# Attention in pairs of query blocks and gate products over the whole array in a hybrid decoder step

## The chip, the cores and the metric

The kernel runs on one core of one Trainium2 chip. The metric is the device time of one execution in microseconds (us). Three runs of the kernel before gave 1314.17, 1315.66 and 1316.99 us (median 1315.66 us).

## What is computed

One step of a hybrid decoder layer, for a prompt of 1024 tokens and eight single new tokens, all in float32. The input is normalised and multiplied with a wide weight `w_in`, and the columns of the product are split up:

```
xn = rms_norm(x, norm_pre)
u, z_rnn, q, k, v, z_attn, g_rnn, g_attn = split(xn @ w_in)
uc = causal_conv(u)                                   # four taps
r, i = sigmoid(uc @ w_a + b_a), sigmoid(uc @ w_x + b_x)   # 16 diagonal blocks of 64 channels
h = linear scan over time of (a(r), b(r, i, uc))
y_rnn = (h * silu(z_rnn)) @ w_rnn_out
for g, (window, dilation) in enumerate(((128, 1), (512, 4), (2048, 16))):
    o[g], lse[g] = dilated causal attention with linear biases, query blocks of 128
y_attn = (merge of o by lse * silu(z_attn)) @ w_attn_out
out = x + rms_norm((sigmoid(g_rnn) * y_rnn + sigmoid(g_attn) * y_attn) @ w_out, norm_post)
```

The eight new tokens go the same way, with caches of keys and values. There are 3 attention groups, 8 heads of 64 channels in each, and 1024 recurrent channels.

## The kernel before, in words

**Projections.** `w_in` is taken in pieces of 128 columns. A projection (`project`, L409) computes one piece for all 1032 tokens in three chunks of 256, 384 and 392 columns (`CHUNKS`). To keep float32 accuracy with the faster fp32r matmul, weights and inputs are split into a high and a low part, and each chunk is 8 x 3 matmuls (`mm3`, L389: high by high, high by low, low by high) into one PSUM tile of the tag `pj`. ScalarE or VectorE reads the chunk out of PSUM (the `evac` functions) and so frees the tile. The weights of the next pieces are loaded by DMAs of 512 KB, issued from SyncE, and split by ScalarE (L225) and VectorE (L226).

**Lanes.** TensorE works through the projections in a fixed order, and other work is slipped in between. That other work is written as Python generators in lanes: the recurrence (`chain`, L601), the attention (L778), its merge, the new tokens (`sample`). The emitting program keeps a clock, `clk`, that adds up what it thinks each matmul costs. After each half of a chunk `tick` (L109) lets every lane whose due time has come emit one step. A step ends with `yield N`, and its lane is due again N ns later. So the order on every engine is set when the program is written out, and each half chunk of 12 matmuls is followed by a visit of some lanes, or of none.

**Slots.** Most SBUF tiles come from an arena of `NSLOT` slots of equal size. Weights are loaded ahead only as far as slots are free. Where a needed slot isn't free, `Arena.get` (L53) forces the lanes on (`force`, L117), due or not, until one is.

**PSUM.** `ps_tile` (L81) gives 8 banks of 512 columns: 3 to `pj`, 3 to `s`, 1 to `pt`, 1 to `o`.

**The gate products** (`chain_front`, L553). For each block of 128 channels and each half `s` of it, the tile `xs[s]` holds 64 channels' high parts on 64 partitions and their low parts on the other 64. The product with the high weights `lh` runs over all 128 partitions; the one with the low weights `ll` uses only the 64 partitions of the high parts. Both add into one `s` tile, and ScalarE takes two sigmoids from it (L591). A step emits all three chunks of one half, six matmuls: 16 such steps in all, four for each of the four chains.

**Attention** (L778). One pass for each group and pair of heads, 12 in all, each over 8 query blocks. `scores` multiplies the queries of a block with one or two key blocks for both heads, each head over its 64 partitions, into two `s` tiles; VectorE adds the bias and takes the minimum (L802), ScalarE the exponential (L806). `turn` transposes the result into a `pt` tile, which is copied out by VectorE or ScalarE (L820, L822). `values` multiplies with the values, each head into 64 output partitions (128 by 64 in the rows). One step does one block: `scores` of block b, `turn` of block b-2, `values` of block b-4, with the first two and two later steps also turning rows of v and k. Steps are 1700 ns of `clk` apart:

```
for b in range(8 + 2 * LAG):
    if LAG <= b < 8 + LAG:
        turn(b - LAG)
    if b < 8:
        scores(b)
    if b >= 2 * LAG:
        values(b - 2 * LAG)
```

Of the kernel before, what the change touches and what calls it, by code (L numbers as in the profile page):

```python
# [22 lines left out]
DIL = (1, 4, 16)  # L23
# [6 lines left out]
NSLOT = 43  # L30
# [3 lines left out]
LAG, STEP = 2, 1700  # L34
# [5 lines left out]
def f32(ap):  # L40
    return ap.bitcast(F32)
# [28 lines left out]
def hybrid_step(ctx: ExitStack, tc: tile.TileContext, I, O):  # L70
# [10 lines left out]
    def ps_tile(tag):  # L81
        bufs = {"pj": 3, "s": 3, "pt": 1, "o": 1}[tag]
        return psum.tile([128, 512], F32, tag=tag, bufs=bufs, name="ps_" + tag)
# [64 lines left out]
    def tr(out, in_, idn):  # L148
        clk[0] += 109
        nc.tensor.transpose(out, in_, idn)  # L150
# [401 lines left out]

    def chain_front(b, X, R, T):  # L553
# [3 lines left out]
        ll = small.tile([128, 256], F32R, tag="t2", name="ll")  # L557
        nc.scalar.activation(lh, lw, AF.Copy)
        nc.vector.tensor_tensor(ll, lw, f32(lh), op=OP.subtract)
# [21 lines left out]
        for s in range(2):  # L581
            rows = slice(64 * s, 64 * s + 64)
            ws = slice(128 * s, 128 * s + 128)
            for c0, n in CHUNKS:
                p = ps_tile("s")
                cs = slice(c0, c0 + n)
                mm(p[:, :n], lh[:, ws], xs[s][:, cs], start=True, stop=False)
                mm(p[:, :n], ll[rows, ws], xs[s][rows, cs], start=False, stop=True)
                for gate in range(2):
                    at = 64 * (gate ^ s)  # L590
                    nc.scalar.activation(G[gate][rows, cs], p[at:at + 64, :n], AF.Sigmoid,  # L591
                                         bias=par[rows, b, 5 + gate:6 + gate])
            yield 1500
# [184 lines left out]
    def attention(g, hp):  # L778
# [14 lines left out]
        def scores(b):  # L793
            k0, n = keys(b)
            pt = P[b] = small.tile([128, 2, 256], F32, tag="P", name="P", bufs=LAG + 1)
            base = C["base2"] if g == 2 else C["base0"][:, 256 - 128 * n:256]
            for h in range(2):
                p = ps_tile("s")
                hs = slice(64 * h, 64 * h + 64)
                mm(p[:, :128 * n], qt[hs, 128 * b:128 * b + 128], kt[hs, 128 * k0:128 * (k0 + n)],  # L800
                                 start=True, stop=True)
                nc.vector.tensor_tensor_reduce(out=pt[:, h, :128 * n], in0=p[:, :128 * n], in1=base,  # L802
                                               scale=-SLOPES[g][2 * hp + h] * DIL[g], scalar=3e38,
                                               op0=OP.add, op1=OP.min, accum_out=st[:, g, 0, h, b:b + 1])
            for h in range(2):
                nc.scalar.activation(pt[:, h, :128 * n], pt[:, h, :128 * n], AF.Exp, scale=-1.0,  # L806
                                     bias=st[:, g, 0, h, b:b + 1], accum_out=st[:, g, 1, h, b:b + 1])

        def turn(b):
            k0, n = keys(b)  # L810
            pt = P.pop(b)
            p = ps_tile("pt")
            for h in range(2):
                for kb in range(n):
                    tr(p[:, (h * n + kb) * 128:(h * n + kb) * 128 + 128],
                                        pt[:, h, 128 * kb:128 * kb + 128], ident)
            t = PT[b] = small.tile([128, 2 * n, 128], F32, tag="PT", name="PT", bufs=LAG + 1)
            src = p[:, :256 * n].rearrange("p (b c) -> p b c", c=128)
            if b % 2:
                nc.vector.tensor_copy(t, src)  # L820
            else:
                nc.scalar.activation(t, src, AF.Copy)  # L822

        def values(b):
            k0, n = keys(b)
            vn = vns[g, hp]
            t = PT.pop(b)
            if b % 4 == 0:
                PO[0] = ps_tile("o")
            o = PO[0]  # L830
            off = 128 * (b % 4)
            for kb in range(n):
                for h in range(2):
                    mm(o[64 * h:64 * h + 64, off:off + 128], vn[:, k0 + kb, 64 * h:64 * h + 64],
                                     t[:, h * n + kb], start=kb == 0, stop=kb == n - 1)
            if b % 4 == 3:
                f = b // 4
# [10 lines left out]
        for b in range(8 + 2 * LAG):  # L848
            if LAG <= b < 8 + LAG:
                turn(b - LAG)  # L850
            if b < 8:
                scores(b)
            if b >= 2 * LAG:
                values(b - 2 * LAG)
            if b < 2:
                v_rows(g, hp, b)
            elif 6 <= b < 8:
                k_rows(g, hp, b - 6)
            if b == 7:
                ar.free(kts.pop((g, hp)), qts.pop((g, hp)))  # L860
            if b == 7 + 2 * LAG:
                ar.free(vns.pop((g, hp)))
                if g == 2:
                    spawn("merge", merge(hp), 1000)
            yield STEP
# [300 lines left out]
    for e in started:  # L1166
        advance(e)
    C = late_consts()
# [219 lines left out]
```

## Time and profile before

| what | value |
|---|---|
| median of the three runs | 1315.66 us |
| the profiled execution's own time | 1316.49 us |
| its span in the profile | 1314.1 us |
| TensorE matmuls (PE) busy | 1294.3 us, 98% |
| TensorE weight loads (PEld) busy | 1203.1 us, 92% |
| VectorE (DVE) busy | 604.8 us, 46% |
| ScalarE (ACT) busy | 550.0 us, 42% |
| GpSimd (POOL) busy | 219.8 us, 17% |
| mean granted TensorE clock | 0.996 |

Matmuls are pipelined, so a row's duration is longer than what it costs: the cost of one in a sequence is the distance between its start and the start of the next. An fp32 product of the attention shows as two rows (two passes), an fp32r product or a transpose as one. What a timeline row merges (x4) is the stretch from its start to the next row's start.

### The profile page before, as it was taken

What the parts mean: (1) busy time and instruction counts of PE and PEld (TensorE: products, weight loads), DVE (VectorE), ACT (ScalarE), POOL (GpSimd) and SP (SyncE); (2) the same over time, 40 slices, a digit from 0 to 9 for tenths busy, and PEclk for the clock granted to TensorE, in tenths of its full rate; (3) what the DMA queues carried; (4) which work ended last, traced back from release to release, by engine and by line L of the source; (5) the groups of instructions that cost most, each with busy time, mean ns of one, the idle gap of its engine ahead of it and who ended that gap; (6) DMA issues with size and microseconds to landing.
All of it is one profiled execution on the core that took longest, in us unless ns stands there. A gap on an engine that the chain in (4) does not pass through costs nothing.

```text
span 1314.1 us, 21425 instructions
## 1 busy us (share of the span) xinstructions
PE 1294.3 (98%) x8726; PEld 1203.1 (92%) x8726; DVE 604.8 (46%) x1300; ACT 550.0 (42%) x1223; POOL 219.8 (17%) x228
## 2 busy tenths in 40 slices
PE   8999999999999999999999999999999999999996
PEld 8998999989998898888988988888989999999996
DVE  6552744827436324533345325544244245555225
ACT  6548357384574343334334333333563222122222
POOL 4001402314022002240016002140026000001001
PEclk9999999999999999999999999999999999999998
DMA  7201300423302017312354115421285356313033
GB/s 237 69 23 33 98 16 17 145 81 131 95 17 89 25 41 206 87 51 65 89 137 102 41 41 169 109 66 45 50 228 158 120 184 211 105 65 98 32 113 146
DMA packets 149303, 125.96 MB, mean 96 GB/s; under 512 B 8857, under 2 KB 135289, under 8 KB 149198
## 3 DMA queue, kind: packets, MB, share of 16 engines
q1 hardware_dynamic: 149206, 124.61, 31.6%
q8 instruction: 68, 1.11, 0.4%
q14 instruction: 29, 0.24, 0.1%
HBM read 98.44 MB, written 26.21 MB: 95 GB/s over the span
## 4 chain that ended last, share of the span: by engine, by line
PE 94%; DVE 2%; ACT 1%; issue 1%; DMA 0%; POOLq 0%; POOL 0%; SPq 0%; ACTq 0%; DVEq 0%
PE ps_pj L146 79%; PE ps_s L146 7%; PE ps_o L146 3%; PE ps_s L150 3%; PE ps_pt L150 2%; DVE ck L1036 1%; ACT P L806 0%; DMA wraw<-in_w_in 0%; DVE wlo L226 0%; DVE tanh L631 0%; ACT whi L225 0%; DVE PT L820 0%; DVE P L802 0%; POOLq L1384 0%; ACT whi L243 0%
## 5 line engine op out<-in xcount | busy, mean ns | idle before, releaser
L146 PE MATMUL ps_pj<-xh,whi 128*128 128x256 f32 (+3 forms) x1760 | 579.1, 329 | 0.0
L146 PE MATMUL ps_pj<-xh,wlo 128*128 128x256 f32 (+3 forms) x1760 | 558.1, 317 | 0.3 <-DVE wlo L239 0.3
L146 PE MATMUL ps_pj<-xl,whi 128*128 128x256 f32 (+3 forms) x1760 | 558.0, 317 | 0.0
L146 PEld LDWEIGHTS ps_pj<-xh,whi 128*128 128x128 f32 x1760 | 331.6, 188 | 22.8 <-issue 20.9
L146 PEld LDWEIGHTS ps_pj<-xl,whi 128*128 128x128 f32 x1760 | 331.8, 189 | 0.2
L146 PEld LDWEIGHTS ps_pj<-xh,wlo 128*128 128x128 f32 x1760 | 331.4, 188 | 0.5 <-DVE wlo L239 0.5
L226 DVE TENSOR_TENSOR wlo<-wraw,whi 128x512 fp32r<-128x512 f32 x176 | 152.5, 867 | 296.3 <-ACT whi L225 285.9
L806 ACT ACTIVATE P<-P,stat 128x128 f32<-128x128 f32 (+1 forms) x192 | 85.0, 443 | 123.9 <-DVE stat L802 123.8
L225 ACT ACTIVATE whi<-wraw 128x512 fp32r<-128x512 f32 x176 | 109.4, 623 | 7.6 <-DVE tanh L632 3.0
L146 PE MATMUL ps_pj<-wlo,mh 128*128 128x256 f32 (+1 forms) x288 | 79.1, 281 | 0.0
L146 PE MATMUL ps_pj<-whi,ml 128*128 128x256 f32 x256 | 72.0, 281 | 0.0
L146 PE MATMUL ps_pj<-whi,mh 128*128 128x256 f32 x256 | 72.0, 281 | 0.0
L802 DVE CUSTOM_DVE_ANT_0 P<-ps_s,base 128x128 f32<-128x128 f32 (+1 forms) x192 | 59.7, 347 | 21.6 <-PE ps_s L146 18.2
L820 DVE COPY PT<-ps_pt 128x512 f32<-128x512 f32 (+1 forms) x48 | 28.8, 600 | 87.8 <-PE ps_pt L150 49.9
L706 ACT ACTIVATE qt<-ps_pj,qsc 128x384 f32<-128x384 f32 (+1 forms) x36 | 27.4, 762 | 94.8 <-PE ps_pj L146 94.8
L146 PE MATMUL ps_s<-kt,qt 64*128 64x128 f32 (+1 forms) x384 | 59.0, 372 | 3.2 <-DVE stat L802 3.2
L146 PE MATMUL ps_pj<-hzl,whi 128*128 128x256 f32 (+2 forms) x192 | 61.5, 320 | 0.0
L146 PE MATMUL ps_pj<-hzh,wlo 128*128 128x256 f32 (+2 forms) x192 | 61.5, 320 | 0.0
L146 PE MATMUL ps_pj<-hzh,whi 128*128 128x256 f32 (+2 forms) x192 | 61.4, 320 | 0.0
L1088 ACT ACTIVATE sg<-ps_pj 128x256 f32<-128x256 f32 (+2 forms) x48 | 21.9, 457 | 92.8 <-PE ps_pj L146 90.8
L591 ACT ACTIVATE gate<-ps_s,par 64x256 f32<-64x256 f32 (+2 forms) x96 | 52.1, 542 | 13.2 <-PE ps_s L146 10.5
L146 PE MATMUL ps_o<-PT,vn 128*64 128x128 f32 x560 | 52.2, 292 | 1.3 <-ACT ot L846 1.3
(243 smaller groups left out, 1679.2 us busy)
## 6 DMA issues: line engine op xcount, KB each, us to landing
wraw<-in_w_in SPq DMA_DIRECT2D x72, 512.0 KB
ck<-in_cache_kv_w SPq DMA_DIRECT2D x24, 512.0 KB
sgd<-sg SPq DMA_DIRECT2D x16, 516.0 KB
sgl<-sgd SPq DMA_DIRECT2D x16, 516.0 KB
xin<-in_x_prompt SPq DMA_DIRECT2D x16, 512.0 KB
qb<-sd SPq DMA_DIRECT2D x12, 512.0 KB
fb<-fd SPq DMA_DIRECT2D x24, 256.0 KB
hzd<-uc SPq DMA_DIRECT2D x8, 516.0 KB
```

Of the source, the lines that this page charges most:

```text
L146: nc.tensor.matmul(out, lhsT, rhs, start=start, stop=stop)
L150: nc.tensor.transpose(out, in_, idn)
L225: nc.scalar.activation(hi[:, a:b], raw[:, a:b], AF.Copy)
L226: nc.vector.tensor_tensor(lo[:, a:b], raw[:, a:b], f32(hi[:, a:b]), op=OP.subtract)
L591: nc.scalar.activation(G[gate][rows, cs], p[at:at + 64, :n], AF.Sigmoid, bias=par[rows, b, 5 + gate:6 + gate])
L706: nc.scalar.activation(dst, src, AF.Copy, scale=C["qsc"][:, g, hp:hp + 1])
L802: nc.vector.tensor_tensor_reduce(out=pt[:, h, :128 * n], in0=p[:, :128 * n], in1=base, scale=-SLOPES[g][2 * hp + h] * DIL[g], scalar=3e38, ...
L806: nc.scalar.activation(pt[:, h, :128 * n], pt[:, h, :128 * n], AF.Exp, scale=-1.0, bias=st[:, g, 0, h, b:b + 1], accum_out=st[:, g, 1, h, ...
L820: nc.vector.tensor_copy(t, src)
L1036: nc.vector.tensor_tensor(acc, acc, t, op=OP.add)
L1088: nc.scalar.activation(z[:, c0:c0 + n], p[:, :n], AF.Sigmoid)
```

## The change

Four things change together. `scores`, `turn` and `values` take two query blocks at a time, and the loop has 6 steps instead of 12, 3400 ns apart instead of 1700; a step's `turn` handles the pair whose scores were made one step earlier (before: two steps earlier). The low gate weights lie in two standing tiles that are zero outside the two 64 by 128 quarters in use (`clear_low_w` zeroes them once), so the low product runs over all 128 partitions. The gate chunks are emitted one by one, with a `yield 1300` after each instead of a `yield 1500` after three. PSUM goes from 3 to 2 banks for `pj` and from 1 to 2 for `pt`, and the arena has 42 slots instead of 43.

```
-NSLOT = 43
+NSLOT = 42
-LAG, STEP = 2, 1700
+STEP = 3400
...
-        bufs = {"pj": 3, "s": 3, "pt": 1, "o": 1}[tag]
+        bufs = {"pj": 2, "s": 3, "pt": 2, "o": 1}[tag]
...
+    low_w = [const.tile([128, 256], F32R, name=f"low_w{i}") for i in range(2)]
...
-        ll = small.tile([128, 256], F32R, tag="t2", name="ll")
+        ll = low_w[b % 2]
         nc.scalar.activation(lh, lw, AF.Copy)
-        nc.vector.tensor_tensor(ll, lw, f32(lh), op=OP.subtract)
+        for s in range(2):
+            rows, ws = slice(64 * s, 64 * s + 64), slice(128 * s, 128 * s + 128)
+            nc.vector.tensor_tensor(ll[rows, ws], lw[rows, ws], f32(lh[rows, ws]), op=OP.subtract)
...
                 mm(p[:, :n], lh[:, ws], xs[s][:, cs], start=True, stop=False)
-                mm(p[:, :n], ll[rows, ws], xs[s][rows, cs], start=False, stop=True)
+                mm(p[:, :n], ll[:, ws], xs[s][:, cs], start=False, stop=True)
                 for gate in range(2):
                     at = 64 * (gate ^ s)
                     nc.scalar.activation(G[gate][rows, cs], p[at:at + 64, :n], AF.Sigmoid,
                                          bias=par[rows, b, 5 + gate:6 + gate])
-            yield 1500
+                yield 1300
...
+        def scores(bs):
+            ps = [ps_tile("s") for _ in range(2)]
+            for b in bs:
+                k0, n = keys(b)
+                off = 256 * (b % 2)
+                for h in range(2):
+                    hs = slice(64 * h, 64 * h + 64)
+                    mm(ps[h][:, off:off + 128 * n], qt[hs, 128 * b:128 * b + 128], kt[hs, 128 * k0:128 * (k0 + n)],
+                       start=True, stop=True)
+            for b in bs:
...
+        pairs = [(2 * i, 2 * i + 1) for i in range(4)]
+        for i in range(6):
+            if 1 <= i < 5:
+                turn(pairs[i - 1])
+            if i < 4:
+                scores(pairs[i])
+            if i >= 2:
+                values(pairs[i - 2])
+            if i < 2:
+                v_rows(g, hp, i)
+            elif i < 4:
+                k_rows(g, hp, i - 2)
...
+            yield STEP
...
+    clear_low_w()
     C = late_consts()
```

How this moves instructions shows at three places.

**TensorE, one visit of the recurrence.** `lh` and `ll` (after: `low_w`) are the high and low gate weights, `uc` the split input. Before, in the last chain:

```order
L146 MATMUL ps_pj<-xh_24_123,wlo_2710 128x256
L146 MATMUL ps_s<-uc_156_2674,lh 128x256
L146 MATMUL ps_s<-uc_156_2674,ll 128x256
L146 MATMUL ps_s<-uc_156_2674,lh 128x384
L146 MATMUL ps_s<-uc_156_2674,ll 128x384
L146 MATMUL ps_s<-uc_156_2674,lh 128x392
L146 MATMUL ps_s<-uc_156_2674,ll 128x392
L146 MATMUL ps_pj<-xh_17_116,whi_2709 128x384
```

After, an ordinary visit in the second chain:

```order
L146 MATMUL ps_pj<-xh_24_123,wlo_2125 128x256
L146 MATMUL ps_s<-uc_120_2090,lh 128x256
L146 MATMUL ps_s<-uc_120_2090,low_w_135 128x256
L146 MATMUL ps_pj<-xh_17_116,whi_2124 128x384
L146 MATMUL ps_pj<-xl_25_124,whi_2124 128x384
```

Six matmuls in one visit become two, in three visits.

**The second chain's end, where the arena has no slot left.** After the change eight pairs stand in a row here, at the end of the last `z` projection, forced by the next projection's weights. On TensorE, the first six of the eight pairs (the last two, of 392 columns, and then the next projection follow):

```order
L146 MATMUL ps_s<-uc_120_2090,lh 128x392
L146 MATMUL ps_s<-uc_120_2090,low_w_135 128x392
L146 MATMUL ps_s<-uc_125_2174,lh 128x392
L146 MATMUL ps_s<-uc_125_2174,low_w_136 128x392
L146 MATMUL ps_s<-uc_121_2091,lh 128x256
L146 MATMUL ps_s<-uc_121_2091,low_w_135 128x256
L146 MATMUL ps_s<-uc_126_2175,lh 128x256
L146 MATMUL ps_s<-uc_126_2175,low_w_136 128x256
L146 MATMUL ps_s<-uc_121_2091,lh 128x384
L146 MATMUL ps_s<-uc_121_2091,low_w_135 128x384
L146 MATMUL ps_s<-uc_126_2175,lh 128x384
L146 MATMUL ps_s<-uc_126_2175,low_w_136 128x384
```

ScalarE's part of the same place, after the change (`zs` reads a `pj` tile, each `gate` row an `s` tile):

```order
L549 ACTIVATE zs_2221<-ps_pj 128x392
L601 ACTIVATE gate_2253<-ps_s,par 64x392
L601 ACTIVATE gate_2254<-ps_s,par 64x392
L601 ACTIVATE gate_2275<-ps_s,par 64x392
L601 ACTIVATE gate_2276<-ps_s,par 64x392
L601 ACTIVATE gate_2253<-ps_s,par 64x256
L601 ACTIVATE gate_2254<-ps_s,par 64x256
L601 ACTIVATE gate_2275<-ps_s,par 64x256
L601 ACTIVATE gate_2276<-ps_s,par 64x256
```

Each `s` tile has two sigmoids to wait for, and there are three such tiles.

**TensorE, one visit of the attention** in the group with dilation 16 (one key block for each query block). Before:

```order
L146 MATMUL ps_pj<-xh_24_123,wlo_4735 128x256
L150 MATMUL ps_pt<-ident,P 128x128 x2
L146 MATMUL ps_s<-kt_4466,qt_4638 128x128 x2
L146 MATMUL ps_o<-PT,vn_4763 64x128 x2
L146 MATMUL ps_pj<-xh_17_116,whi_4734 128x384
L146 MATMUL ps_pj<-xl_25_124,whi_4734 128x384
```

After (here with a step that also turns rows of k):

```order
L146 MATMUL ps_pj<-xh_20_119,wlo_4720 128x384
L150 MATMUL ps_pt<-ident,P 128x128 x4
L146 MATMUL ps_s<-kt_4450,qt_4606 128x128 x4
L146 MATMUL ps_o<-PT,vn_4755 64x128 x4
L150 MATMUL ps_s<-ident,kt_4450 128x128 x4
L146 MATMUL ps_pj<-xh_21_120,whi_4719 128x384
```

Each visit holds twice the products, and there are half as many visits. Between two of one pass stand 24 to 36 projection matmuls after the change, 12 to 24 before.

## Rows read from the trace of the kernel before

**Rows 1.** Page, part 1: busy us (share) x instructions.
```profile
PE 1294.3 (98%) x8726; PEld 1203.1 (92%) x8726; DVE 604.8 (46%) x1300; ACT 550.0 (42%) x1223; POOL 219.8 (17%) x228
```

**Rows 2.** TensorE timeline, one gate visit: start us, us, line, out<-in, shape, xcount.
```profile
270.19 0.28 PE L146 MATMUL ps_s<-uc,lh 128*128 128x256 f32 x1
270.40 0.38 PE L146 MATMUL ps_s<-uc,ll 64*128 64x256 f32 x1
270.71 0.44 PE L146 MATMUL ps_s<-uc,lh 128*128 128x384 f32 x1
...
272.21 0.44 PE L146 MATMUL ps_pj<-xh,whi 128*128 128x384 f32 x1
272.49 0.34 PE L146 MATMUL ps_pj<-xl,whi 128*128 128x384 f32 x1
```

**Rows 3.** TensorE timeline, an attention visit with one key block.
```profile
501.62 0.34 PE L146 MATMUL ps_pj<-xh,wlo 128*128 128x392 f32 x1
501.80 0.38 PE L150 MATMUL ps_pt<-ident,P 128*128 128x128 f32 x2
502.11 0.49 PE L146 MATMUL ps_s<-kt,qt 64*128 64x128 f32 x4
502.53 0.44 PE L146 MATMUL ps_o<-PT,vn 128*64 128x128 f32 x4
502.90 0.39 PE L146 MATMUL ps_pj<-xh,whi 128*128 128x256 f32 x1
503.12 0.27 PE L146 MATMUL ps_pj<-xl,whi 128*128 128x256 f32 x1
503.23 0.28 PE L146 MATMUL ps_pj<-xh,wlo 128*128 128x256 f32 x1
```

**Rows 4.** TensorE timeline, an attention visit with two key blocks.
```profile
909.74 0.60 PE L150 MATMUL ps_pt<-ident,P 128*128 128x128 f32 x4
910.27 0.70 PE L146 MATMUL ps_s<-kt,qt 64*128 64x256 f32 x4
910.90 0.66 PE L146 MATMUL ps_o<-PT,vn 128*64 128x128 f32 x8
911.49 0.44 PE L146 MATMUL ps_pj<-xh,whi 128*128 128x384 f32 x1
911.77 0.34 PE L146 MATMUL ps_pj<-xl,whi 128*128 128x384 f32 x1
```

**Rows 5.** Timeline around 606.8 us, weight load (PEld) beside matmul.
```profile
606.77 0.19 PEld L146 LDWEIGHTS ps_pj<-xh,wlo 128*128 128x128 f32 x1
606.89 0.28 PE L146 MATMUL ps_pj<-xh,wlo 128*128 128x256 f32 x1
```

**Rows 6.** Page, part 5: busy us, mean ns of one | idle before.
```profile
L591 ACT ACTIVATE gate<-ps_s,par 64x256 f32<-64x256 f32 (+2 forms) x96 | 52.1, 542 | 13.2 <-PE ps_s L146 10.5
```

**Rows 7.** VectorE timeline, projections of `za`.
```profile
232.58 4.32 DVE L631 TENSOR_TENSOR_SCAN tanh<-gate,sq 128x1024 f32<-128x1024 f32 x1
...
255.46 0.42 DVE L677 TENSOR_TENSOR za<-ps_pj,za 128x256 f32<-128x256 f32 x1
```

**Rows 8.** TensorE timeline, the chunk two after the one read in rows 7.
```profile
251.65 0.34 PE L146 MATMUL ps_pj<-xh,whi 128*128 128x392 f32 x1
```

**Rows 9.** Timeline, all engines, one attention visit: scores, then ScalarE's exponentials.
```profile
607.89 0.70 PE L146 MATMUL ps_s<-kt,qt 64*128 64x256 f32 x4
...
609.67 0.49 ACT L806 ACTIVATE P<-P,stat 128x256 f32<-128x256 f32 x1
```

**Rows 10.** TensorE timeline around its longest wait in the attention.
```profile
862.98 0.60 PE L150 MATMUL ps_pt<-ident,P 128*128 128x128 f32 x4
865.47 1.44 PE L146 MATMUL ps_s<-kt,qt 64*128 64x256 f32 x4 [1.88 <-DVE stat L802]
...
867.88 0.70 PE L146 MATMUL ps_pj<-xh,whi 128*128 128x392 f32 x1
```

**Rows 11.** VectorE timeline of the same stretch.
```profile
861.66 3.40 DVE L1036 TENSOR_TENSOR ck<-ck,ck 128x1024 f32<-128x1024 f32 x1
```

More of the change, by code (lines that the diff above doesn't have):

```diff
@@ L551, in proj_z, with clear_low_w @@
         return project(evac)
+    low_w = [const.tile([128, 256], F32R, name=f"low_w{i}") for i in range(2)]
+    def clear_low_w():
+        for t in low_w:
+            for q in range(2):
+                nc.gpsimd.tensor_scalar(t[:, 128 * q:128 * q + 128], ident, 0.0, None, op0=OP.mult)
     def chain_front(b, X, R, T):
@@ L791, in keys @@
             return (b, 1)
[L793 to L813, printed above, removed]
-                for kb in range(n):
[L815 to L837, printed above, removed]
+        def scores(bs):
[8 more added lines that the diff above has]
+            for b in bs:
+                k0, n = keys(b)
+                off = 256 * (b % 2)
+                pt = P[b] = small.tile([128, 2, 256], F32, tag="P", name="P", bufs=2)
+                base = C["base2"] if g == 2 else C["base0"][:, 256 - 128 * n:256]
+                for h in range(2):
+                    nc.vector.tensor_tensor_reduce(out=pt[:, h, :128 * n], in0=ps[h][:, off:off + 128 * n], in1=base,
+                                                   scale=-SLOPES[g][2 * hp + h] * DIL[g], scalar=3e38,
+                                                   op0=OP.add, op1=OP.min, accum_out=st[:, g, 0, h, b:b + 1])
+                for h in range(2):
+                    nc.scalar.activation(pt[:, h, :128 * n], pt[:, h, :128 * n], AF.Exp, scale=-1.0,
+                                         bias=st[:, g, 0, h, b:b + 1], accum_out=st[:, g, 1, h, b:b + 1])
@@ new lines, in turn @@
+        def turn(bs):
+            for b in bs:
+                k0, n = keys(b)
+                pt = P.pop(b)
+                p = ps_tile("pt")
+                for h in range(2):
+                    for kb in range(n):
+                        tr(p[:, (h * n + kb) * 128:(h * n + kb) * 128 + 128],
+                           pt[:, h, 128 * kb:128 * kb + 128], ident)
+                t = PT[b] = small.tile([128, 2 * n, 128], F32, tag="PT", name="PT", bufs=4)
+                src = p[:, :256 * n].rearrange("p (b c) -> p b c", c=128)
+                if b % 2:
+                    nc.vector.tensor_copy(t, src)
+                else:
+                    nc.scalar.activation(t, src, AF.Copy)
@@ new lines, in values @@
+        def values(bs):
+            vn = vns[g, hp]
+            for b in bs:
+                k0, n = keys(b)
+                t = PT.pop(b)
+                if b % 4 == 0:
+                    PO[0] = ps_tile("o")
+                o = PO[0]
+                off = 128 * (b % 4)
+                for kb in range(n):
+                    for h in range(2):
+                        mm(o[64 * h:64 * h + 64, off:off + 128], vn[:, k0 + kb, 64 * h:64 * h + 64],
+                           t[:, h * n + kb], start=kb == 0, stop=kb == n - 1)
+            if bs[-1] % 4 == 3:
+                f = bs[-1] // 4
+                o = PO[0]
@@ L846, in values @@
                 nc.scalar.activation(dst, src, AF.Copy)
[L848 to L859, printed above, removed]
+        pairs = [(2 * i, 2 * i + 1) for i in range(4)]
[10 more added lines that the diff above has]
+                k_rows(g, hp, i - 2)
+            if i == 3:
                 ar.free(kts.pop((g, hp)), qts.pop((g, hp)))
-            if b == 7 + 2 * LAG:
+            if i == 5:
                 ar.free(vns.pop((g, hp)))
```

## The prediction

> **What bounds the kernel now.** I read the page's first part, then TensorE's timeline. TensorE shows a matmul under way for 1294.3 of 1314.1 us [rows 1]; no engine beside it is over half busy. So what counts is how far apart matmuls start, and the reader is to see in the timeline where that distance is longer than the columns need. Between projection matmuls it is 0.11 to 0.12 us for 256 columns and 0.18 for 392 [rows 3], and I take 0.18 for 384. Around a product that uses half the partitions, or half the output partitions, it is longer.
>
> Compare a visit with one key block [rows 3] with one with two [rows 4]. The scores take 0.42 us (502.11 to 502.53) and with twice the columns 0.63 (910.27 to 910.90): 0.21 is work, so 0.21 of the 0.42 is fixed. The values take 0.37 (502.53 to 502.90) and with twice the products 0.59 (910.90 to 911.49): 0.22 is work, 0.15 fixed. Two transposes before scores take 0.31 and four take 0.53: 0.11 each, 0.09 fixed. The first projection matmul after the visit takes 0.22 instead of 0.12 (502.90 to 503.12), or 0.28 instead of 0.18 [rows 4]: 0.10 fixed. These four amounts are paid once for each visit, however much is in it. I read them as the price of changing which part of the array is used: the pipeline runs empty, and the first weights load uncovered.
>
> A gate visit changes back and forth three times: the six products and the slow first matmul after them take 2.02 + 0.10 = 2.12 us (270.19 to 272.21, 272.21 to 272.49) [rows 2]. At undisturbed distances six products are 2 x (0.12 + 0.18 + 0.18) = 0.96. Even the high product, over all partitions, takes 0.21 for 256 columns when a low one follows, and that low one 0.31 [rows 2].
>
> **The gains.** The low product over the whole array streams the same columns, so only the changes of mode go: 2.12 - 0.96 = 1.16 us for each of 16 visits, **18.6 us**. That the chunks are now spread out costs nothing by itself, since all three products on either side use the whole array.
>
> In attention one pass of before enters the half-array modes 12 times (8 scores steps, 4 steps with values alone), has 8 score and 8 value stages and returns 12 times. The change halves each. Saved in a pass: 6 entries x 0.09, 4 x 0.21, 4 x 0.15 and 6 returns x 0.10, or 0.54 + 0.84 + 0.60 + 0.60 = 2.58 us; for 12 passes **31.0 us**. Within a merged stage nothing fixed should be added, as two heads and two key blocks stand in one stage now without it [rows 4]. Together 49.6 us.
>
> The Trainium skill, "TensorEngine Tiling (Array Packing)", Key Properties, says that changing the tiling mode drains TensorE. The rows agree, but show more than a drain: with the 0.09 alone at each of the 96 + 168 changes saved, the gain would be 24 us.
>
> **The losses.** (a) With 42 slots and longer gate steps, the arena runs out at the end of the last z projection, and eight gate pairs stand in a row. They take 2.6 us of TensorE, but there are three `s` tiles and each is freed by two sigmoids of 0.54 us [rows 6]. The eighth pair waits for the fifth pair's sigmoids, the tenth in the queue: 5.4 us and half a microsecond for the z chunk that ScalarE reads first, plus the pair itself, 0.36. Loss 5.9 + 0.4 - 2.6 = 3.7; bounds 2 (sigmoids begun early) and 7 (all sixteen awaited). I take **3.6**, as part of the first pair's wait lies beside the pair.
>
> (b) Two `pj` banks instead of three: chunk c+2 may start only when chunk c has been read. In the za projections VectorE is behind: one chunk was read until 255.88 (start 255.46 plus 0.42) [rows 7], while the chunk two later started at 251.65 [rows 8], 4.2 us too early for two banks. What VectorE does there is the recurrence, such as a scan that takes 4.32 us [rows 7]. The lag of one such stretch is paid once, since TensorE, when it waits, lets VectorE catch up. The change moves the chains' ends by some projections, partly to the gate projections, which need no VectorE to be read, and partly onto other z and za projections, and the second chain's end is forced there with the slots. I take **6** (the worst lag, and half of it again for the other stretches); bounds 0 (the ends clear every projection read by VectorE) and 12 (three such stretches).
>
> (c) The last chain's gates now lie among the attention's first visits: twelve pairs bring ScalarE 24 sigmoids x 0.54 = 13 us where its exponentials already stand. I take **3**; bounds 0 and 10, by the price of (a) and of (b).
>
> (d) Waits in attention. Scores to transposes: the second head's exponential starts 1.8 us after the scores and takes 0.49 [rows 9]. With two more exponentials the last ends about 3.3 us after. In the order after the change 24 projection matmuls at least stand between two visits, and where it is 24 they have 384 or 392 columns: 24 x 0.18 = 4.3 us, plus the values. So transposes are covered by a microsecond or more. Scores need the `s` tiles of the visit before. That failed once for long: four transposes, 0.44, scores, 0.63, and values, 0.59, took 4.90 us (862.98 to 867.88) [rows 10], since VectorE stood in an addition of 3.40 us [rows 11]. The distance between visits grows, which helps; the tiles wait for four reads instead of two, which hurts. I take **0**, bounds -5 and +12 (a quarter microsecond for each of 48 visits).
>
> (e) The rest: VectorE's eight low-weight subtractions are cut in two, the four clearings on GpSimd stand long before their use, values follow their transposes by one step of 3400 instead of two of 1700; each lies under an engine that is half idle, or the projections of a chunk; if uncovered, they would show as waits of (c) and (d). New-token and merge matmuls that shared visits now have some ten of their own, at 0.09 to 0.2 each: **1**. No DMA is added; loads issue up to a projection later for want of slots, which costs nothing while a projection (11 us) lies between a load and its use; (b)'s upper bound holds a late one.
>
> Sum: 49.6 - 3.6 - 6 - 3 - 0 - 1 = 36 us. From the profiled execution's own 1316.5 that gives 1280.5; it stands 0.8 above the median of the runs, and I round up to **1281**. (A change under 0.2%, 2.6 us, can't be told from none.)
>
> **The rivals.**
> 1. *No new waits.* (b) to (d) vanish because TensorE's neighbours have slack [rows 1]: 1316.5 - 49.6 + 3.6 + 1 = 1271. For it: every wait is local. Against it: the lag in rows 7 and 8. Chance 0.13.
> 2. *Attention waits.* The cover between a visit's scores and its successor fails regularly, (c) and (d) at their upper bounds: 1281 + 7 + 12 = 1300. For it: the lag of one step instead of two, rows 10. Chance 0.12.
> 3. *Loads of the padded weights lie open.* The low product now uses the same rows of the array as the high one. If its load could not lie under the product before, 96 products would cost 0.11 more each (the fixed 0.21 of the scores less an entry of 0.10): 10.6 us back, 1292. Against it: in projections, which use the same rows throughout, a load starts with the product before (606.77) and its own product follows 0.12 later [rows 5]. Chance 0.02. The Trainium skill, "TensorE: Matmul & The Clock Gate", Part 3, The mechanism, says that loads overlap with matmuls under way only when the row groups differ; by that, this rival. The projections' rows disagree.
> 4. *The visits don't merge the cost*: each block inside a merged stage pays its fixed part again. Then only the gates gain: 1316.5 - 18.6 + 13.6 = 1311. Against it: rows 4. Chance 0.03.
> 5. *Slower: two projection banks bind everywhere.* If ScalarE's queue, with four exponentials in a row, delays reading of chunks past the next chunk's length, TensorE stalls at each chunk. Some 116 chunks stand beside attention. It decides where they wait 36 / 116 = 0.31 us each; at 0.6 it gives 1281 + 116 x 0.6 = 1351. Against it: ScalarE is 42% busy [rows 1], and four exponentials of 0.5 us are less than the shortest chunk, 24 x 0.12 = 2.9. Chance 0.03.
>
> **How the numbers follow.** The forecast, gains whole and losses within their bounds, has 0.67. Its own range is 1271 to 1293. To hold 8 in 10 the range takes in most of rivals 1 and 3 and half of rival 2: **1269 to 1298**. Faster: all but rival 5 and a small chance that several losses meet at their bounds: 0.95; same 0.02; slower 0.03.
>
> **What would show it.** Right: gate products 0.12 or 0.18 us apart with no slow matmul after them; scores of two blocks in about 0.63 us for one key block each, values in 0.59, at half as many visits. TensorE's waits, near none now, would show for `s` after the sigmoids in one stretch at the last z projection, and for `pj` on the sigmoid or product of z and za. Wrong: slow first passes inside a merged stage (rival 4), a low product 0.1 us late (rival 3), or idle time before projection matmuls all through attention (rival 5).

## The result, and the profile after

The changed kernel takes **1292.92 us** (median of 4 runs, 1290.66 to 1295.04) against 1315.33 for the kernel before beside it (1314.17 to 1316.99): a ratio of 0.9828, with a 95% interval from 0.9807 to 0.9849. It is faster by 22.4 us. The forecast was 34 us; the time lies in the range, 12 us above the predicted 1281. The profiled execution took 1292.06.

The gains came as the rows of before had promised. TensorE's timeline of the change: a gate visit, then an attention visit of two blocks with two key blocks each, then one of two blocks with one key block each; the columns are those of [rows 2]:

```profile
107.63 0.34 PE L146 MATMUL ps_s<-uc,lh 128*128 128x384 f32 x1
107.81 0.34 PE L146 MATMUL ps_s<-uc,low_w 128*128 128x384 f32 x1
107.98 0.34 PE L146 MATMUL ps_pj<-xh,whi 128*128 128x384 f32 x1
108.16 0.34 PE L146 MATMUL ps_pj<-xl,whi 128*128 128x384 f32 x1
...
407.65 1.04 PE L150 MATMUL ps_pt<-ident,P 128*128 128x128 f32 x8
408.62 1.13 PE L146 MATMUL ps_s<-kt,qt 64*128 64x256 f32 x8
409.68 1.09 PE L146 MATMUL ps_o<-PT,vn 128*64 128x128 f32 x16
410.71 0.39 PE L146 MATMUL ps_pj<-xh,whi 128*128 128x256 f32 x1
...
501.75 0.60 PE L150 MATMUL ps_pt<-ident,P 128*128 128x128 f32 x4
502.28 0.71 PE L146 MATMUL ps_s<-kt,qt 64*128 64x128 f32 x8
502.92 0.66 PE L146 MATMUL ps_o<-PT,vn 128*64 128x128 f32 x8
```

A gate product now stands 0.18 us before its neighbour, and the projection matmul after it too; the 0.31 and 0.28 of [rows 2] are gone. Eight score rows take 0.64 (502.28 to 502.92), as four rows of twice the columns did before [rows 4]; eight score rows of twice the columns take 1.06 (408.62 to 409.68) and sixteen value rows 1.03 (409.68 to 410.71). Of the distances beyond the columns' work, one 0.21 and one 0.15 are left for each visit.

What was lost shows in the waits of TensorE. The columns: engine, tile and line, what it waited for, us in total, times, the longest. First the three of the kernel before that do not belong to its opening (a fourth is 0.3 us), then the five costliest of the changed one.

```profile
PE ps_s L146 <- DVE stat L802: 3.2, 3, 1.9
PE ps_o L146 <- ACT ot L846: 1.3, 1, 1.3
PE ps_pt L150 <- DVE PT L820: 1.2, 1, 1.2
```

```profile
PE ps_pj L146 <- DVE za L687: 10.3, 5, 4.9
PE ps_pj L146 <- ACT whi L225: 2.5, 1, 2.5
PE ps_pt L150 <- ACT P L823: 2.3, 2, 2.2
PE ps_s L146 <- ACT gate L601: 1.9, 4, 0.7
PE ps_pj L146 <- DVE on L1363: 1.5, 1, 1.5
```

Before, the three lines all belong to attention. After, they have gone, one for `P` has come, and the others are outside attention: projections waited for `za` to be read, once for a high weight, and in the last stage for `on`; the burst of gate pairs waited for `gate`. The waits are not the whole of the loss. Busy time by stretch, in four stretches: the end of the burst and what follows it, and behind the three longest waits (start and end, us, busy time of each engine, PEclk the granted clock as a share of 2.4 GHz, DMA share, GB/s):

```profile
215.30:221.90 6.60, 6.44 (x24) 5.45 (x25) 0.00 (x0) 6.39 (x11) 2.06 (x1) 0.50 0.00 0
242.60:249.20 6.60, 4.15 (x13) 4.15 (x14) 6.46 (x7) 0.00 (x0) 2.76 (x1) 0.50 0.00 0
263.00:266.20 3.20, 3.20 (x12) 3.20 (x11) 3.12 (x6) 0.00 (x0) 0.00 (x0) 0.50 0.56 163
1177.80:1184.40 6.60, 6.21 (x27) 5.92 (x28) 2.41 (x4) 1.71 (x5) 0.00 (x0) 0.50 0.93 312
```

In each TensorE ran at 1.2 GHz. The kernel before had one stretch of 3.4 us of the kind in mid-program, behind its wait of 1.88 [rows 10].

**The account.** TensorE's timeline has the first matmul of the first `za` projection, and that of the gate projection after the four of `za`: 288 matmuls.

```profile
218.24 0.41 PE L146 MATMUL ps_pj<-xh,whi 128*128 128x256 f32 x1
...
280.32 0.28 PE L146 MATMUL ps_pj<-xh,whi 128*128 128x256 f32 x1
```

They took 62.1 us. The same two in the timeline of the kernel before:

```profile
221.96 0.28 PE L146 MATMUL ps_pj<-xh,whi 128*128 128x256 f32 x1
...
267.36 0.28 PE L146 MATMUL ps_pj<-xh,whi 128*128 128x256 f32 x1
```

That is 45.4, or 96 matmuls each at 0.12, 0.18 and 0.18. So za lost **16.7 us**: 10.3 of waits, and most of the rest the slow clock. Added up from the distances between matmuls, 1.7 us of it are the slow clock behind the burst, and the four long waits, with what follows each, come to 1.6, 7.1, 1.2 and 4.6. Three further losses, in TensorE's timeline of the change:

```profile
211.26 0.34 PE L146 MATMUL ps_s<-uc,lh 128*128 128x392 f32 x1
...
213.08 0.38 PE L146 MATMUL ps_s<-uc,lh 128*128 128x256 f32 x1 [0.70 <-ACT gate L601]
214.28 0.45 PE L146 MATMUL ps_s<-uc,lh 128*128 128x384 f32 x1 [0.71 <-ACT gate L601]
...
1175.22 0.28 PE L146 MATMUL ps_pj<-whi,ml 128*128 128x256 f32 x1
1178.05 0.58 PE L146 MATMUL ps_pj<-whi,mh 128*128 128x256 f32 x1 [2.55 <-ACT whi L225]
...
1269.60 0.38 PE L146 MATMUL ps_pj<-whi,mh 128*128 128x256 f32 x1 [1.51 <-DVE on L1363]
```

The burst of eight gate pairs runs from 211.26 to 218.24, 7.0 us for 2.6 of work: **4.4** lost. The output weights: 2.83 from 1175.22 to 1178.05 where 0.12 is the distance, and then 27 matmuls in 6.4 us (1178.05 to 1184.49) where 3.2 would do: **6.0** by the distances. The last stage: about **1.8** with the slow first pass behind the wait. Together 28.9. The profiled times differ by 1316.5 - 1292.06 = 24.4, so against gains of 49.6 some 25.2 is lost net, and about 4 was gained beyond the forecast. That 4 is a remainder and no reading; attention's old waits, 5.7 us in the three lines above, are the likely source.

### The profile page after: what moved, and what is told of

The parts are those of the page before. It is cut to its first block, busy times and chain, and to the rows that moved or that the text cites. A ratio compares the mean times of both kernels' runs of the same rounds, so it can differ in the third digit from the quotient of the medians.

```text
span 1290.3 us, 21474 instructions
## 1 busy us (share of the span) xinstructions
PE 1256.5 (97%) x8726; PEld 1207.8 (94%) x8726; DVE 602.0 (47%) x1308; ACT 553.1 (43%) x1229; POOL 222.5 (17%) x232
## 4 chain that ended last, share of the span: by engine, by line
PE 86%; ACT 5%; DVE 5%; issue 2%; DMA 1%; POOL 0%; POOLq 0%; SPq 0%; DVEq 0%; ACTq 0%
PE ps_pj L146 74%; PE ps_s L146 5%; PE ps_o L146 3%; PE ps_s L150 3%; PE ps_pt L150 2%; DVE wlo L226 1%; ACT gate L601 1%; DVE tanh L641 1%; ACT whi L225 1%; DVE ck L1057 1%; ACT gate L623 1%; DMA wraw<-in_w_in 0%; ACT sq L627 0%; ACT P L823 0%; DVE on L1326 0%
## 5 line engine op out<-in xcount | busy, mean ns | idle before, releaser
L146 PE MATMUL ps_pj<-xh,whi 128*128 128x256 f32 (+3 forms) x1760 | 573.3, 326 | 11.4 <-DVE za L687 10.3
L226 DVE TENSOR_TENSOR wlo<-wraw,whi 128x512 fp32r<-128x512 f32 x176 | 146.6, 835 | 321.9 <-ACT whi L225 316.0
L819 DVE CUSTOM_DVE_ANT_0 P<-ps_s,base 128x128 f32<-128x128 f32 (+1 forms) x192 | 56.0, 348 | 9.0 <-PE ps_s L146 8.5
L840 ACT ACTIVATE PT<-ps_pt 128x256 f32<-128x256 f32 (+1 forms) x48 | 21.0, 437 | 91.0 <-PE ps_pt L150 90.9
L146 PEld LDWEIGHTS ps_pj<-whi,mh 128*128 128x128 f32 x256 | 49.5, 193 | 4.5 <-ACT whi L225 2.8
L146 PEld LDWEIGHTS ps_pj<-wlo,mh 128*128 128x128 f32 (+1 forms) x288 | 52.3, 182 | 0.5 <-DVE wlo L226 0.4
```

The source lines that it names most:

```text
L146: nc.tensor.matmul(out, lhsT, rhs, start=start, stop=stop)
L226: nc.vector.tensor_tensor(lo[:, a:b], raw[:, a:b], f32(hi[:, a:b]), op=OP.subtract)
```

## The experiments

All times are medians; "before" is the kernel before run beside them (1314.2 to 1315.0), the interval is that of the ratio. Where two kernels from different sets of runs are compared, their medians are subtracted; counted against the "before" beside each, such a difference comes out up to 1.1 us otherwise.

**1. Does each half give what the rows promised, and what do two banks cost alone?**

`gates_alone`: the kernel before, with

```diff
         ll = small.tile([128, 256], F32R, tag="t2", name="ll")
         nc.scalar.activation(lh, lw, AF.Copy)
-        nc.vector.tensor_tensor(ll, lw, f32(lh), op=OP.subtract)
+        for s in range(2):
+            nc.gpsimd.tensor_scalar(ll[:, 128 * s:128 * s + 128], ident, 0.0, None, op0=OP.mult)
+        for s in range(2):
+            rows, ws = slice(64 * s, 64 * s + 64), slice(128 * s, 128 * s + 128)
+            nc.vector.tensor_tensor(ll[rows, ws], lw[rows, ws], f32(lh[rows, ws]), op=OP.subtract)
...
-                mm(p[:, :n], ll[rows, ws], xs[s][rows, cs], start=False, stop=True)
+                mm(p[:, :n], ll[:, ws], xs[s][:, cs], start=False, stop=True)
```

> The kernel before with one thing of the change: the low gate weights padded with zeros to the whole array (in the small tiles they stood in, zeroed again for each block, so that 43 slots fit); three chunks a step, three projection banks, single query blocks. Theory: only the 1.16 us of each of 16 gate visits goes, 18.6 us, and nothing else moves: 1296.7 us, between 1294.5 and 1299. Rival (the gain is smaller because the padded loads lie open or the visits were hidden): 1307.

Measured 1305.51 (0.9929, 0.9915 to 0.9942): 9.4 us, half of the theory's, and near the rival's number for neither of its reasons. TensorE's timeline of one visit's second and third pair shows where most of the rest went:

```profile
277.71 0.34 PE L146 MATMUL ps_s<-uc,lh 128*128 128x384 f32 x1
277.88 0.34 PE L146 MATMUL ps_s<-uc,ll 128*128 128x384 f32 x1
278.75 0.45 PE L146 MATMUL ps_s<-uc,lh 128*128 128x392 f32 x1 [0.53 <-ACT gate L596]
```

The products are as quick as forecast, but the third pair waits for an `s` tile that ScalarE is still reading. The old 1.16 us of mode changes had hidden that. Ten of the 16 visits show it; the mean visit takes 1.30 us, not 0.96, which is 5.4 of the missing 9.2. Another 3.7 lie at the za projections (49.1 us instead of 45.4); TensorE's waits name `za` (1.9) and a low weight (0.9) there, and I did not follow them further. With the next kernel they were gone as well (45.7).

`gates_twos`: as `gates_alone`, with a step of two chunks.

```diff
-            for c0, n in CHUNKS:
+            for ci, (c0, n) in enumerate(CHUNKS):
...
-            yield 1500
+                if (3 * s + ci) % 2:
+                    yield 1300
```

> The kernel before with padded low weights (zeroed again for each block, 43 slots) and gate steps of two chunks; three projection banks, single query blocks. Theory (the padding is worth 18.6 us, and with steps of three chunks 5.7 of it went into waits for the gate tiles' sigmoids): 1297 us, between 1294 and 1300. Rival (what was missing with steps of three lies elsewhere, at the za projections): 1304.

1296.74 (0.986, 0.9843 to 0.9877): 18.3 us, the forecast's 18.6 within the interval (16.2 to 20.6). So emitting gate chunks apart belongs to the padding.

`pairs_alone`: the attention of the change and its bank numbers, with the gates and the 43 slots of before.

```diff
-NSLOT = 42
+NSLOT = 43
...
-        ll = low_w[b % 2]
+        ll = small.tile([128, 256], F32R, tag="t2", name="ll")
...
-                mm(p[:, :n], ll[:, ws], xs[s][:, cs], start=False, stop=True)
+                mm(p[:, :n], ll[rows, ws], xs[s][rows, cs], start=False, stop=True)
...
-                yield 1300
+            yield 1500
```

> The attention half of the change alone: two query blocks a step with two projection and two transpose banks, 43 slots, the gates as before. Theory: 31 us for the merged visits, some 5 more because the attention stalls of before go, less some 5 for two banks at the za projections (a 4 us lag of VectorE and the slower clock after it): 1284 us, between 1279 and 1288. Rival (two banks themselves cost the 16 us that the changed kernel lost at its za projections, in whatever order the gates come): 1295.

1286.84 (0.9786, 0.9771 to 0.9801): 28.1 us.

`banks_alone`: the kernel before with the bank numbers of the change.

```diff
-        bufs = {"pj": 3, "s": 3, "pt": 1, "o": 1}[tag]
+        bufs = {"pj": 2, "s": 3, "pt": 2, "o": 1}[tag]
```

> The kernel before with two projection and two transpose banks, nothing else. Theory: the lag of VectorE at the za projections is paid once, 4 us, with the slower clock behind it 3 more; the second transpose bank is worth 1 or 2: 1320 us, between 1316 and 1324. Rival (two banks bind by themselves): 1331.

1324.41 (1.007, 1.0056 to 1.0083): 9.5 us slower, a little above the theory's range. Its waits hold those of [rows 7, 8] and one that nobody had named, in the last stage:

```profile
PE ps_pj L146 <- DVE zs L550: 2.4, 3, 2.0
PE ps_pj L146 <- DVE za L677: 2.2, 3, 1.0
PE ps_pj L146 <- DVE on L1341: 1.5, 1, 1.5
```

Its longest wait, 2.0 us for `zs`, has its cause in ScalarE: its read of the chunk stood behind a table load of 1.28 us, two exponentials and a second table load, and VectorE had been idle 4.77 us when it got the chunk. So two banks are too few for ScalarE's queue as well as VectorE's.

With these 9.5 taken out, the merged visits alone are worth 28.1 + 9.5 = 37.6 us: the forecast's 31.0 and 6.6 more, about what the attention waits that went with them amount to. That is a difference of two runs, not a run, and its split is not shown.

**2. What made za so dear: two banks, the order of the gates, or the slot?**

`threes_43`: the change with gate steps of three chunks and 43 slots.

```diff
-NSLOT = 42
+NSLOT = 43
...
-        ll = low_w[b % 2]
+        ll = small.tile([128, 256], F32R, tag="t2", name="ll")
...
+        for s in range(2):
+            nc.gpsimd.tensor_scalar(ll[:, 128 * s:128 * s + 128], ident, 0.0, None, op0=OP.mult)
...
-                yield 1300
+            yield 1500
```

> The changed kernel with the gates again in steps of three chunks and with 43 slots (the padded low weights stand in the small tiles): nothing is forced for want of slots any more, the second chain ends where it did before. Pairs, padding and two banks stay. Theory (the order of the gate steps made the burst, put the chain's tail onto the za projections and the weights late): the burst's 4.7, about 11 of the 16 us at za and the 6 us at the first out projection come back: 1269 us, between 1264 and 1274. Rival (two banks cost that at za in any order): the burst and the out projection alone, 1282.

1277.48 (0.9716, 0.97 to 0.9731). It is 37.4 us faster than before, and `gates_alone` and `pairs_alone` sum to 37.5: within the noise the halves do not disturb each other. It lies above the theory's range, which counted 18.6 for the gates; in steps of three they are worth 9.4.

`change_43`: the same 43 slots, but with the change's gates one by one (the last piece of the diff left out).

> The change with 43 slots instead of 42 (the padded low weights stand in the small tiles and are zeroed again for each block); gates one by one, pairs, two banks. In its order eight gate chunks are still forced in a row at the end of the last z projection, but the second chain's tail is not, and the first two pieces of the output weights are loaded one projection earlier. Theory (three separate losses: burst, tail on the za projections, late weights): the late weights' 6 us come back and some of za's, the burst stays: 1284 us, between 1279 and 1288. Rival (the lost slot is the cause of all of it): 1277, as with steps of three chunks.

1275.92 (0.9708, 0.9689 to 0.9727). My theory falls: one slot, with the place where the low weights stand, is worth **17 us** of the change's 25 (16 against the "before" beside each). The two were changed together and not tried apart. The burst is still there (four waits for `gate`, below). What went is the high weight's wait and half of za's:

```profile
PE ps_pj L146 <- DVE za L683: 4.7, 2, 3.2
PE ps_s L146 <- ACT gate L597: 1.9, 4, 0.7
```

Its two ends of the za projections, in TensorE's timeline:

```profile
219.81 0.42 PE L146 MATMUL ps_pj<-xh,whi 128*128 128x256 f32 x1
...
273.41 0.28 PE L146 MATMUL ps_pj<-xh,whi 128*128 128x256 f32 x1
```

53.6 us, 8.5 less than in the change, and still 8.2 more than before. With the weights' 6.0 the 8.5 make 14.5 of the 17; the remaining 2.5 are about what the change waited for `P` (2.3), a line that is gone too. Of the change's four long waits at za, those of 4.93 and 0.94 us have gone (7.1 and 1.2 us with what followed them); those of 1.39 and 2.84 stand here as 1.52 and 3.16. So the slot took half of what za lost; the other half is there without it.

VectorE's timeline of the change shows what the missing slot did there:

```profile
235.02 0.57 DVE L687 TENSOR_TENSOR za<-ps_pj,za 128x392 f32<-128x392 f32 x1 [4.59 <-ACT za L686]
...
243.97 0.68 DVE L226 TENSOR_TENSOR wlo<-wraw,whi 128x512 fp32r<-128x512 f32 x1
244.58 0.42 DVE L687 TENSOR_TENSOR za<-ps_pj,za 128x256 f32<-128x256 f32 x1
```

The chain's next steps had been forced into one row, because a weight's tile had no slot: six operations of the recurrence (235.50 to 244.05), and then the low weight, stand before the read that TensorE waits for (4.93 us). In `change_43` reads and weights stand between those operations.

The first row is another matter: VectorE had been idle for 4.59 us when it got that chunk. ScalarE's timeline of the change shows why:

```profile
229.85 1.28 ACT L627 ACT_TABLE_LOAD   x1
...
233.19 1.28 ACT L686 ACT_TABLE_LOAD   x1
234.49 0.50 ACT L686 ACTIVATE za<-ps_pj 128x392 f32<-128x392 f32 x1
```

The chain's two square roots (2.03 us), and a table load on either side of them, stood before ScalarE's read of the chunk. That is the wait of 1.39 us, and `change_43` has it too.

`change_42_wide`: the change with 42 slots, in which projections also use the two `pt` banks outside attention.

```diff
+    wide, turns = [False], [0]
...
+        if tag == "pj" and wide[0]:
+            tag = ("pj", "pt")[turns[0] // 2 % 2]
+            turns[0] += 1
         bufs = {"pj": 2, "s": 3, "pt": 2, "o": 1}[tag]
...
+    wide[0] = True
...
+    wide[0] = False
     for hp in range(4):
         for g in range(3):
...
     until(lambda: not lanes)
+    wide[0] = True
```

> The change as it is, 42 slots, but projections use the two transpose banks as well outside attention. Theory (the forced chain makes VectorE late by more than two banks cover; four cover it): the 10 us of waits at za, the 1.5 at the end and some 4 of the slower clock after those waits come back, the burst and the late output weights stay: 1277 us, between 1272 and 1282. Rival (the forced tail reaches further than four banks, only slots help): 1288.

1281.32 (0.9749, 0.973 to 0.9769), at the upper end of the theory. In the profiled execution, which took 1285.93, the waits for `za` are all gone, but others stand in their place (first line; the second is the late output weight, as in the change):

```profile
PE ps_pt L151 <- DVE wlo L231: 5.2, 3, 2.5
...
PE ps_pt L151 <- ACT whi L230: 2.6, 1, 2.6
```

Four banks let TensorE run on until it needs the low weight, which is in the same queue of VectorE behind the same forced chain. So banks hide the late read, and not the late weight. The waits for `P`, in attention, are 4.4 us here against the change's 2.3.

`threes_42`: the change with steps of three, 42 slots (the diff of the step alone).

> The change with steps of three gate chunks, 42 slots and two banks kept: the fourth corner beside the change (one by one, 42), the same with 43 slots, and steps of three with 43. In its order two gate steps are forced at the eighth z projection's start, no tail; the first output weights come a projection late. Theory (the slot costs 6 us of late weights in any order, and the 11 us more that it cost the change were the forced tail of its longer chain): 1277.5 + 6 + 1 = 1285 us, between 1281 and 1288. Rival (the slot costs its 17 us in any order): 1294.

1282.19 (0.9756, 0.9731 to 0.9781), as the theory said: with the shorter chain the slot costs 4.7 us, with the longer one 17. It shows the wait for `whi` again (2.7), but za's waits are 1.4 in all. So half of what is lost at za takes the slot and the order together; the late output weights take the slot alone.

**3. Was the second transpose bank needed?**

`threes_43_pj3`: `threes_43` with `"pj": 3` and `"pt": 1`.

> The kernel with steps of three gate chunks and 43 slots, with three projection banks and one transpose bank again. Theory: the 8 us that projections lose at z and za and the 1.5 at the end come back, but the second block of each pair can be transposed only when the first block's copy has left the one bank, which costs 0.5 to 0.9 us at each of 48 visits: 1277.5 - 9 + 34 = 1302 us, between 1290 and 1314. Rival (the second transpose bank was not needed, since a copy is short): 1268.

1303.98 (0.9917, 0.9901 to 0.9932): 26.5 us more than `threes_43`, as the theory had it. One line of TensorE's waits holds most of it:

```profile
PE ps_pt L150 <- ACT PT L836: 26.0, 48, 0.8
```

48 waits of 0.54 us, the second block of each pair for the copy of the first. A visit's transposes then take, for one, 1.22 us instead of 0.53; 48 such differences are 33 us, of which the third projection bank gave some 7 back. The pairs do need the bank that the projections gave up.

**4. Can both be had?**

`threes_43_wide`: `threes_43` with the banks of `change_42_wide`.

> The kernel with steps of three gate chunks and 43 slots, where projections use the two transpose banks as well before attention starts and from the output projections on: four banks where z and za are read. Theory: the waits for VectorE at z and za (8 us) and the 1.5 us at the end vanish: 1268 us, between 1265 and 1271. Rival (VectorE's lag there is longer than two more banks, and moves to the next projections): 1275.

1266.52 (0.9634, 0.9616 to 0.9651): 11.0 less: the waits for `zs`, `za` and `on`, 9.4 us in `threes_43`, are all gone, and 2.2 for a low weight have come.

`twos_43_wide`: the same with gate steps of two chunks, as in `gates_twos`.

> As the one before, with the gates in steps of two chunks: no chunk is forced, and in a visit the third pair no longer waits for the sigmoids of the pairs before. In steps of three a gate block's two visits take 1.30 us in the mean against 0.94 for three pairs one by one. Theory: 2 to 5 us of the 5.7 come back on top: 1264 us, between 1261 and 1268. Rival (longer gate steps delay the chain as in the change): 1272 or more.

**1260.15** (0.9581, 0.9564 to 0.9598), 54 us faster than before and 33 than the change, the fastest here. Of the six lines in its view of TensorE's waits four belong to the opening; the other two are of 0.3 us each, for `l` and for a low weight.

`twos_42_wide`: the same with 42 slots and the change's `low_w` tiles.

> The fastest so far (steps of two gate chunks, four banks outside attention) with 42 slots and the change's own low weight tiles: five gate steps and two later ones are forced for want of a slot, and the output weights load a projection late. Theory (the slot is worth the late weights' 6 us, and the forced steps cost little with four banks and steps of two): 1266 us, between 1263 and 1270. Rival (a lost slot costs the 17 us that it costs in the change): 1277.

1271.5 (0.9666, 0.9652 to 0.968), between theory and rival: the slot costs 11.3. The late weights are there (`whi`, 2.7), and five forced steps make a burst of their own behind the eighth z projection; TensorE's timeline shows waits for `gate` of 0.68 and 0.58 us among others.

I had taken forced steps for cheap with four banks. They are not: the gates' tiles are `s`, and those are still three.

## Why the prediction was right, and where it was wrong

Its likeliest case held in the total: the gains came whole, and the time lies at the upper edge of that case's own range (1271 to 1293). One loss, (b), lay above its bound. The sum was 36, the profile gives 24.4. The 11.6 between them are two errors of opposite sign: the burst, the banks and the late weights took 28.9 where (a) and (b) had 9.6, and (c) to (e), put at 4 of loss, came out as some 4 of gain. That the second made up for 8 us of the first was luck.

- **Gains of the gates, 18.6:** right. 18.3 in `gates_twos`; in the change 39 of the 40 pairs outside the burst stand at their columns' distance. The step that called the spread of chunks free was right, but not for its reason: without it the sigmoids would take half of the gain.
- **Gains of attention, 31.0:** right in mechanism, by the distances of the merged stages; the size agrees as far as a difference of runs shows it (37.6 with the waits that went). (d), the attention's waits, came out near its good bound.
- **(a) The burst, 3.6:** 4.4; the sigmoids' sum was right, the slow clock in it was not counted. That it needs the lost slot was wrong: `change_43` has the same burst with 43. It comes with the longer chain.
- **(b) Two banks, 6 (0 to 12):** alone 9.5. In the change, za lost 16.7 and the last stage 1.8, beyond the upper bound. The step that failed is "the lag of one such stretch is paid once, since TensorE, when it waits, lets VectorE catch up". TensorE paid four times, with waits of 1.39, 4.93, 0.94 and 2.84 us, and not for one lag. The first is ScalarE's, behind its table loads, and the prediction had looked at VectorE alone. The second and third are the forced tail: VectorE had six operations, then a scan of 4.14 us and one of 4.21 (starts 244.91 and 250.29) between one read and the next, so a wait did not let it catch up. The fourth is the lag that the prediction had read in [rows 7, 8], the next chain's first steps, and cost 4.6 in all. The prediction said that the second chain's end is forced there and priced it by a stretch of before, in which nothing was forced; that tail cost 8.3 of the 16.7.
- **"Loads issue up to a projection later, which costs nothing":** the second failed step. The first output blocks need two pieces of weights at once, and the second was issued only as they began (1173.93; their first matmul starts at 1173.91). SyncE's timeline has it as the first of five:

```profile
1173.93 4.57 SPq L207 DMA_DIRECT2D wraw<-in_w_out  x5
```

ScalarE could begin to convert it 3.4 us later, at 1177.37, after 1.52 us for nothing but this transfer. The 11 us "between a load and its use" that the prediction set against it are not there where two pieces are used together. Cost: 6.0. In `change_43` that piece was issued a projection earlier, and the wait is gone.
- **(c) The last chain among attention's visits, 3:** the size was near, the cause another. Its gate pairs stand at their columns' distance, so the sigmoids cost nothing. But at 454.82 the transposes waited 2.16 us for `P`: VectorE reached those scores only at 452.61. It had been idle for 3.75 us until ScalarE, held by a table load (1.28 us) and the chain's square roots (2.02), had made a high weight; then a step of the chain (1.23) stood before the scores, among others. ScalarE then began with a second table load (1.28, from 452.98) before the exponential. The prediction had counted sigmoids and no table loads.
- **The clock** is in none of the terms. Behind each of three long stoppages, and in the burst, came 3 to 7 us at 1.2 GHz; a wait of 2.55 us cost 6.0 in all, and za's 10.3 of waits, with the burst's clock, 16.7. Bounds made of lags alone were too small for that.

Of the rivals, none came. What rival 1 supposed, no new waits, needed four banks and 43 slots (1266.5 and 1260.2). Rival 3 gave 1292, the measured time, for a reason that is not there: padded products stand 0.12 and 0.18 us apart, with no load open. The Trainium skill, "TensorE: Matmul & The Clock Gate", Part 3, The mechanism, says in one line that loads overlap only where row groups differ, and further up in the same section that a load into a background weight buffer is pulled ahead as well; the trace of the change disagrees with the first, as the projections of before did [rows 5]. A right time is no proof of a mechanism.

## What to carry to other kernels

When a change makes a product faster, ask what its slowness had hidden: here some 0.3 us of waiting for the next accumulator at each visit (1.30 us instead of 0.96). Where a planner issues work early for want of memory, price the row of forced operations in every queue in which a read or a weight stands behind it, ScalarE's table loads included; a tile's worth of memory was here worth 17 us with one order of the gates and 5 with another. A stoppage of TensorE can cost its length and a stretch at half clock behind it: 2.55 us of wait were worth 6.0.

## What the runs showed of the hardware

VectorE's operations took longer beside GpSimd's than the forecast had seen. In `change_43` the two scans of one chain stand close together in VectorE's timeline, and GpSimd's timeline shows its product:

```profile
250.74 2.27 DVE L637 TENSOR_TENSOR_SCAN tanh<-gate,sq 128x1024 f32<-128x1024 f32 x1
...
254.26 4.18 DVE L637 TENSOR_TENSOR_SCAN tanh<-gate,sq 128x1024 f32<-128x1024 f32 x1
```

```profile
253.89 2.40 POOL L643 TENSOR_TENSOR uc<-tanh,zs 128x1032 f32<-128x1032 f32 x1
```

The first scan, with GpSimd idle from 250.54 on, took 2.27 us; the second began while a GpSimd product ran to 256.29, and took 4.18: the 2.03 until then and 2.15. So the scan of [rows 7], 4.32 us from 232.58, was by the same reading a scan of 2.3 us that waited: GpSimd's timeline of before has a product until 234.75.

```profile
232.34 2.41 POOL L627 TENSOR_TENSOR sq<-sq,uc 128x1032 f32<-128x1032 f32 x1 [3.92 <-DVE sq L625]
```

The Trainium skill, "SBUF — State Buffer", SBUF: two separate sides, says that, where a VectorE instruction has two inputs in SBUF and the GpSimd one reads SBUF too, whichever of the two starts first holds their shared ports for the whole instruction, and the other blocks; these rows agree. In the change four operations of VectorE at za, starting at 239.98, 244.91, 250.29 and 255.15 while a GpSimd product ran, took 2.74, 4.14, 4.21 and 2.77 us, where their like took 0.70, 2.27, 2.27 (the scan above) and 0.68 without one: 7.9 us together, and the first of them stands before the read that made TensorE wait 4.93. The kernel before had such pairs too, and three banks hid them. No run here took the GpSimd products away, so what the kernel would gain by it stays open.

Open too is what a stoppage must be like for the slow clock to follow. Waits of 4.93, 2.84 and 2.55 us brought it, as did one of 1.88 in the kernel before; those of 1.39 and 0.94 among the same projections did not, nor did that of 2.16 at 454.82, and the burst, which stood for 0.7 us at a time, did.
